# The FFN blocks of f-tiles 16 and 17: seven block products with one pair in place of the plain output product

## The chip, the cores and the metric

The kernel runs on one core of one Trainium2 chip, as one launch. The metric is the device time of that launch in microseconds (us). TensorE is called PE (PEld is its weight load), VectorE DVE, ScalarE ACT, GpSimd POOL and SyncE SP, as the profile calls them.

## The reference, cut to what matters

```python
def swiglu(x, w_in, w_out):
    gate, up = jnp.split(x @ w_in, 2, axis=-1)
    return (jax.nn.silu(gate) * up) @ w_out
...
        x = x + 0.5 * swiglu(rmsnorm(x, ffn1_norm_g[l]), ffn1_w_in[l], ffn1_w_out[l])
...
        x = x + 0.5 * swiglu(rmsnorm(x, ffn2_norm_g[l]), ffn2_w_in[l], ffn2_w_out[l])
    return rmsnorm(x, final_norm_g)
```

There are 1024 tokens, d_model is 1024 and d_ff is 2816, which is 22 tiles of 128 (the f-tiles). Between the two FFNs stands a mixer (mLSTM and a gated MLP) that the change does not touch. All of it is float32.

## The kernel before

Every float32 matrix product is made of three matmuls: each operand is split into a rounded high part and a low part (a cast on ACT, then a subtraction on DVE), and high*high, high*low and low*high are summed in PSUM (`PROD`, `prod`, `split`, `unit`).

An FFN works on the tokens in two halves of 512. Its input product uses, for each f-tile, a scheme with seven block products instead of eight over the 2x2 blocks of (input rows, gate or up) and (input rows, token half). `group(f)` does the five that are left once `first_products` has done two and put them into DRAM; `fetch` brings these back. Four of its sums of weight blocks run on POOL (lines 303 to 305 and 352). It ends with the activated tile for both token halves, `u3` and `c22`.

The output product goes block by block (`BLOCKS`): four blocks of four f-tiles (0 to 15), one of two (16 and 17), and one of four (18 to 21). Blocks with f0 under `FAST` = 16 use seven block products as well: f-tiles are taken in pairs, `group` of the odd tile makes seven operands of the pair (`H`), and `down_fast` runs for each d of 0 to 3 (output tiles d and d+4) the seven products 11, t1, t2, 21, t3, 22, t4, each over two pairs, so 6 matmuls. On the way, the bank of product 11 is copied to a second bank (line 398) into which t2 accumulates, that one is copied to a third (line 408) into which t3 accumulates, and the results leave by ACT copies (lines 404, 412, 427) and DVE additions (418, 422). Each result is added to the residual in DRAM by an accumulating DMA that POOL issues: 16 of 256 KB for a block.

The block (16, 2) is not under `FAST`: `group` only splits `u3` and `c22`, and `down` computes each of the 16 output tiles plainly, with 2 f-tiles times 3 matmuls, an ACT copy (line 440) and the same kind of accumulating DMA (line 441). The last block (18 to 21) goes to `last`, which makes the final sums.

`run` calls the output product of a block after the first group of the next block. So between group 17 and the products of (16, 2) on PE stands group 18, of 60 matmuls, and after them come groups 19, 20 and 21, of 60 each.

The order on each engine is not the order of the code: a scheduler sets it when the program is built, and at run time each engine goes through its own list in order. Tiles come from rotating pools: four raw weight buffers (`raws`), four split weight units (`fw`), eleven [128, 512] temporaries (`tps`), six PSUM banks "mm". A buffer is written again once its last reader is done; an input that an accumulating DMA reads is free when that DMA has landed. The raw loads of a group or a block are issued by SP.

Of the kernel before, what the change touches and what calls it, by code (L numbers as in the profile page):

```python
# [8 lines left out]
F32 = mybir.dt.float32  # L9
F32R = mybir.dt.float32r  # L10
AF = mybir.ActivationFunctionType
ALU = mybir.AluOpType

P = 128
S = 1024
D = 1024
NH = 512
KT = D // P
DFF = 2816
NF = DFF // P  # L20
BLOCKS = [(0, 4), (4, 4), (8, 4), (12, 4), (16, 2), (18, 4)]
FAST = 16
SPAD = 40
MPAD = 24
TMP = 11
# [9 lines left out]
def block_body(ctx, tc, x, ffn1_norm_g, ffn1_w_in, ffn1_w_out, mix_norm_g, w_mix_in, mlstm_conv_w,  # L35
               mlstm_conv_b, mlstm_b_igate, mlstm_b_fgate, mlstm_head_norm_g, sgu_norm_g, sgu_norm_b,
               sgu_w_s, sgu_b_s, w_mix_out, ffn2_norm_g, ffn2_w_in, ffn2_w_out, final_norm_g, out):
    nc = tc.nc
    V, A, PE, G = nc.vector, nc.scalar, nc.tensor, nc.gpsimd
    x = x[0]  # L40
    out = out[0]
# [4 lines left out]
    raws = []  # L46
# [8 lines left out]
    def bank(tag):  # L55
        return psum[tag].tile([P, NH], F32, tag=tag, name=tag)
# [40 lines left out]
    for nm, src in (("g1", ffn1_norm_g), ("gm", mix_norm_g), ("g2", ffn2_norm_g), ("hg", mlstm_head_norm_g),  # L97
                    ("sg", sgu_norm_g), ("sb", sgu_norm_b), ("cb", mlstm_conv_b)):
        n = src.shape[-1] // P
# [47 lines left out]
    def spread():  # L147
        if todo:
            todo.pop(0)()
# [118 lines left out]
    class Ffn:  # L268
# [60 lines left out]
        def group(self, f):  # L329
# [31 lines left out]
            u3 = sg1  # L361
            if f >= FAST:
                self.hs.append((self.part(self.hp, u3), self.part(bigp, c22)))
# [19 lines left out]
            split(src, t)  # L383
            return t

        def down_fast(self, f0, H, acc):
            for d in range(4):
                r = raws[-1].tile([P, 4, 2, P], F32, tag="raw", name="raw")
                for j in range(2):
                    nc.sync.dma_start(out=r[:, :, j, :], in_=self.w_out[f0 * P:(f0 + 4) * P, (4 * j + d) * P:(4 * j + d + 1) * P]  # L390
                                      .rearrange("(k p) c -> p k c", p=P))
                rv = r.rearrange("p (i s) j c -> p i s j c", s=2)
                a11, a12, a21, a22 = rv[:, :, 0, 0, :], rv[:, :, 1, 0, :], rv[:, :, 0, 1, :], rv[:, :, 1, 1, :]
                w = self.unit(a11, 2)
                a = bank("mm")
                self.prod(a, w, H["11"], True, False)
                x = bank("mm")
                A.copy(out=x, in_=a)
                s1 = self.sums(V, a11, a12, a21, a22, 2)
                w = self.unit(s1, 2)  # L400
                b = bank("mm")
                self.prod(b, w, H["t1"], True, True)
                p5 = self.c512()
                A.copy(out=p5, in_=b)
                w = self.unit(a11, 2)
                self.prod(x, w, H["t2"], False, True)
                y = bank("mm")
                A.copy(out=y, in_=x)
                w = self.unit(a12, 2)
                self.prod(a, w, H["21"], False, True)  # L410
                c11 = self.c512()
                A.copy(out=c11, in_=a)
                G.dma_start(out=acc[0][d], in_=c11, accum_op=ALU.add)  # L413
                V.tensor_tensor(out=a12, in0=a12, in1=a11, op=ALU.subtract)
                w = self.unit(a21, 2)
                self.prod(y, w, H["t3"], False, True)
                c22 = self.c512()
                V.tensor_tensor(out=c22, in0=y, in1=p5, op=ALU.add)  # L418
                G.dma_start(out=acc[1][d + 4], in_=c22, accum_op=ALU.add)
                w = self.unit(a12, 2)  # L420
                self.prod(x, w, H["22"], False, True)
                V.tensor_tensor(out=p5, in0=x, in1=p5, op=ALU.add)
                G.dma_start(out=acc[1][d], in_=p5, accum_op=ALU.add)
                w = self.unit(a22, 2)
                self.prod(y, w, H["t4"], False, True)
                c21 = self.c512()
                A.copy(out=c21, in_=y)
                G.dma_start(out=acc[0][d + 4], in_=c21, accum_op=ALU.add)

        def down(self, f0, n, hs, acc):  # L430
            for d in range(0, KT, 2):
                raw = raws[-1].tile([P, n, 2 * P], F32, tag="raw", name="raw")
                nc.sync.dma_start(out=raw, in_=self.w_out[f0 * P:(f0 + n) * P, d * P:(d + 2) * P]
                                  .rearrange("(k p) c -> p k c", p=P))
                for j in range(2):
                    w = self.unit(raw[:, :, j * P:(j + 1) * P], n)
                    for t in range(2):
                        o = self.down_mm(w, n, [h[t] for h in hs], slice(0, NH))
                        xt = self.c512()
                        A.copy(out=xt, in_=o)  # L440
                        G.dma_start(out=acc[t][d + j], in_=xt, accum_op=ALU.add)
                spread()

        def down_mm(self, w, n, hs, ts):
            o = bank("mm")[:, ts]
# [34 lines left out]
        def run(self, src, final, parts, hook):  # L480
            pend = None
            self.fetch(0)
            for bi, (f0, n) in enumerate(BLOCKS):
                hs = self.hs = []
                H = self.H = {k: [] for k in ("11", "21", "22", "t1", "t2", "t3", "t4")}
                for f in range(f0, f0 + n):
                    self.group(f)
                    if pend is not None:
                        pend()
                        pend = None  # L490
                    spread()
                if f0 < FAST:
                    pend = lambda f0=f0, H=H: self.down_fast(f0, H, src)
                elif bi < len(BLOCKS) - 1:
                    pend = lambda f0=f0, n=n, hs=hs: self.down(f0, n, hs, src)
                else:
                    self.last(f0, n, hs, src, final, parts, hook)

# [387 lines left out]
    with f1:  # L886
# [62 lines left out]
        xt = []  # L949
# [125 lines left out]
```

## Time and profile before

| | us |
|---|---|
| median of 3 runs | 2279.01 (2276.77 to 2283.1) |
| the profiled execution | 2283.09 |
| its span | 2281.3 |
| PE busy in the span | 2230.2 (98%) |
| DVE busy | 1488.2 (65%) |
| ACT busy | 1123.0 (49%) |
| POOL busy | 506.3 (22%) |

The span runs from the first to the last instruction of the profiled execution; the launch itself adds 1.8 us. Busy time of PE is that of modelled, pipelined matmuls, so full PE is read best from the starts of matmuls that follow each other. Idle time of an engine that nothing waits for costs nothing.

### The profile page before, as it was taken

Reading aid. Unit: us, or ns where it says so; the run is one execution under the profiler, and the core shown is the slowest. Engines: PE = TensorE matmul, PEld = TensorE weight load, DVE = VectorE, ACT = ScalarE, POOL = GpSimd, SP = SyncE. Lnnn points to the kernel's source line nnn. Section 1 sums busy time; section 2 is a strip of 40 time slices with the busy share of each in tenths; the row PEclk is TensorE's granted clock in tenths of the full one; section 3 lists DMA queues with packets and bytes.
Section 4 is the critical chain, followed back from the end, with each engine's and each line's share of the span. In section 5 each row is a group of like instructions: output and inputs, shape, how many; then the busy total and the mean of one; then the engine's idle time right before and its main releaser. Section 6 shows DMA issues by size and latency. Waiting matters only on the chain. (4 is left out here: it accounts for less than half of the span.)

```text
span 2281.3 us, 30658 instructions
## 1 busy us (share of the span) xinstructions
PE 2230.2 (98%) x10979; PEld 1868.4 (82%) x10979; DVE 1488.2 (65%) x2563; ACT 1123.0 (49%) x1924; POOL 506.3 (22%) x557
## 2 busy tenths in 40 slices
PE   7999999999999999999999999999999999999998
PEld 5888788788879888888889888888788787878877
DVE  6748777686565757656656576555726786877456
ACT  6645555544534446454434554543644555555542
POOL 3342534424520000000000000000215334253430
PEclk8999999999999999999999999999999999999999
DMA  8853756737753234233343253333864557375663
GB/s 274 268 180 101 154 115 157 135 106 147 176 194 100 77 92 129 84 92 85 101 146 95 84 166 85 91 92 126 269 198 147 111 141 154 97 161 109 149 159 111
DMA packets 331512, 311.51 MB, mean 137 GB/s; under 512 B 19160, under 2 KB 279896, under 8 KB 331360
## 3 DMA queue, kind: packets, MB, share of 16 engines
q1 hardware_dynamic: 292608, 217.20, 32.2%
q0 software_dynamic: 38752, 92.36, 18.5%
q8 instruction: 86, 1.41, 0.3%
q14 instruction: 66, 0.54, 0.1%
HBM read 223.48 MB, written 86.02 MB: 136 GB/s over the span
## 5 line engine op out<-in xcount | busy, mean ns | idle before, releaser
L297 PE MATMUL mm<-b,fw 128*128 128x512 f32 x2640 | 605.6, 391 | 9.6 <-ACT mm L342 4.9
L297 PEld LDWEIGHTS mm<-b,fw 128*128 128x128 f32 x2640 | 496.6, 188 | 116.7 <-ACT mm L342 7.4
L162 PE MATMUL mm<-xn,w 128*128 128x512 f32 x2304 | 546.6, 391 | 0.0
L291 DVE TENSOR_TENSOR fw<-raw,fw 128x512 fp32r<-128x512 f32 (+1 forms) x472 | 328.7, 703 | 297.4 <-ACT fw L290 295.7
L162 PEld LDWEIGHTS mm<-xn,w 128*128 128x128 f32 x2304 | 427.1, 188 | 82.8
L290 ACT CAST fw<-raw 128x512 fp32r<-128x512 f32 (+1 forms) x472 | 248.3, 527 | 174.3 <-PE mm L297 139.1
L297 PE MATMUL mm<-h,fw 128*128 128x512 f32 x1344 | 313.6, 393 | 5.2 <-DVE c L418 4.4
L297 PEld LDWEIGHTS mm<-h,fw 128*128 128x128 f32 x1344 | 248.5, 188 | 68.9 <-ACT fw L290 8.3
L138 DVE TENSOR_TENSOR w<-raw,w 128x1024 fp32r<-128x1024 f32 (+3 forms) x160 | 178.5, 1116 | 163.9 <-ACT w L137 163.4
L297 PE MATMUL mm<-xn,fw 128*128 128x512 f32 x1056 | 246.2, 394 | 3.6 <-ACT xn L195 2.1
L137 ACT CAST w<-raw 128x1024 fp32r<-128x1024 f32 (+3 forms) x160 | 153.9, 964 | 178.8 <-PE mm L162 85.6
L297 PEld LDWEIGHTS mm<-xn,fw 128*128 128x128 f32 x1056 | 199.5, 190 | 49.1 <-ACT xn L195 3.7
L176 PE MATMUL mm<-w,xn 128*128 128x256 f32 x1344 | 163.9, 282 | 0.0
L176 PEld LDWEIGHTS mm<-w,xn 128*128 128x128 f32 x1344 | 161.8, 189 | 1.4 <-issue 0.5
L256 POOL DMA_DIRECT2D xs<-t x16 | 8.7, 544 | 641.8 <-DVE t L253 641.1
L195 ACT CAST h<-c 128x512 fp32r<-128x512 f32 x136 | 82.4, 621 | 73.4 <-DVE c L371 17.6
L196 DVE TENSOR_TENSOR h<-c,h 128x512 fp32r<-128x512 f32 x136 | 101.8, 776 | 10.0 <-ACT h L195 8.9
L303 POOL TENSOR_TENSOR s<-raw 128x512 f32<-128x512 f32 x44 | 62.7, 1424 | 156.5 <-DMA raw<-in_ffn_w_in_dram 121.8
L448 PE MATMUL mm<-h,wl 128*128 128x512 f32 (+1 forms) x480 | 95.9, 353 | 0.0
L413 POOL DMA_DIRECT2D xd<-c x32 | 28.0, 876 | 298.9 <-ACT fw L290 262.2
L162 PE MATMUL po<-mh,w 128*128 128x512 f32 x384 | 87.5, 389 | 0.0
L448 PEld LDWEIGHTS mm<-h,wl 128*128 128x128 f32 x480 | 77.3, 189 | 12.0 <-ACT h L195 0.5
(258 smaller groups left out, 2625.4 us busy)
## 6 DMA issues: line engine op xcount, KB each, us to landing
raw<-in_ffn_w_in_dram SPq DMA_DIRECT2D x264, 256.0 KB, 3.4
raw<-in_w_mix_in_dram SPq DMA_DIRECT2D x96, 512.0 KB, 3.7
xd<-c POOLq DMA_DIRECT2D x160, 256.0 KB, 5.3
eb<-early POOLq DMA_DIRECT2D x88, 256.0 KB, 2.8
c<-eb SPq DMA_DIRECT2D x88, 256.0 KB, 5.2
raw<-in_ffn_w_out_dram SPq DMA_DIRECT2D x72, 256.0 KB, 3.2
raw<-in_w_mix_in_dram SPq DMA_DIRECT2D x32, 384.0 KB, 3.5
xl<-xd POOLq DMA_DIRECT2D x32, 256.0 KB, 4.1
```

The lines of the kernel that those rows point to most:

```text
L137: A.copy(out=w[:, 0, 0:n, :], in_=raw[:, 0:n, :])
L138: V.tensor_tensor(out=w[:, 1, 0:n, :], in0=raw[:, 0:n, :], in1=w[:, 0, 0:n, :].bitcast(F32), op=ALU.subtract)
L162: PE.matmul(out=banks[j], lhsT=w[:, a, i, j * P:(j + 1) * P], rhs=act[k][:, b, ts], start=(k == first and pi == 0), stop=(k == last and pi ...
L176: PE.matmul(out=o, lhsT=act[k][:, b, t * P:(t + 1) * P], rhs=w[:, a, i, :], start=(t % 2 == 0 and k == 0 and pi == 0), stop=(t % 2 == 1 an ...
L195: A.copy(out=dst[:, 0, :], in_=src)
L196: V.tensor_tensor(out=dst[:, 1, :], in0=src, in1=dst[:, 0, :].bitcast(F32), op=ALU.subtract)
L290: A.copy(out=w[:, 0], in_=src)
L291: V.tensor_tensor(out=w[:, 1], in0=src, in1=w[:, 0].bitcast(F32), op=ALU.subtract)
L297: PE.matmul(out=bank, lhsT=w[:, x, i, :], rhs=t[:, y, :], start=(start and i == 0 and pi == 0), stop=(stop and i == len(b) - 1 and pi == 2 ...
L303: G.tensor_tensor(out=s1, in0=a21, in1=a22, op=ALU.add)
L413: G.dma_start(out=acc[0][d], in_=c11, accum_op=ALU.add)
L448: PE.matmul(out=o, lhsT=w[:, x, i, :], rhs=hs[i][:, y, ts], start=(i == 0 and pi == 0), stop=(i == n - 1 and pi == 2))
```

## The change

`FAST` becomes 18, so the block of f-tiles 16 and 17 takes the path of the first four blocks, with one pair: `down_fast` gets the number of f-tiles `n`, its weight units hold n // 2 blocks (128x128 instead of 128x256 where n is 2), and each of the seven products has 3 matmuls. `down` goes away. `group` of f-tile 17 makes the seven operands of the pair where it split two tiles.

```diff
-FAST = 16
+FAST = 18
...
-        def down_fast(self, f0, H, acc):
+        def down_fast(self, f0, n, H, acc):
             for d in range(4):
-                r = raws[-1].tile([P, 4, 2, P], F32, tag="raw", name="raw")
+                r = raws[-1].tile([P, n, 2, P], F32, tag="raw", name="raw")
                 for j in range(2):
-                    nc.sync.dma_start(out=r[:, :, j, :], in_=self.w_out[f0 * P:(f0 + 4) * P, (4 * j + d) * P:(4 * j + d + 1) * P]
+                    nc.sync.dma_start(out=r[:, :, j, :], in_=self.w_out[f0 * P:(f0 + n) * P, (4 * j + d) * P:(4 * j + d + 1) * P]
                                       .rearrange("(k p) c -> p k c", p=P))
...
-                w = self.unit(a11, 2)
+                w = self.unit(a11, n // 2)
...
-                s1 = self.sums(V, a11, a12, a21, a22, 2)
-                w = self.unit(s1, 2)
+                s1 = self.sums(V, a11, a12, a21, a22, n // 2)
+                w = self.unit(s1, n // 2)
...
-        def down(self, f0, n, hs, acc):
-            for d in range(0, KT, 2):
...
-                    w = self.unit(raw[:, :, j * P:(j + 1) * P], n)
-                    for t in range(2):
-                        o = self.down_mm(w, n, [h[t] for h in hs], slice(0, NH))
-                        xt = self.c512()
-                        A.copy(out=xt, in_=o)
-                        G.dma_start(out=acc[t][d + j], in_=xt, accum_op=ALU.add)
...
                 if f0 < FAST:
-                    pend = lambda f0=f0, H=H: self.down_fast(f0, H, src)
-                elif bi < len(BLOCKS) - 1:
-                    pend = lambda f0=f0, n=n, hs=hs: self.down(f0, n, hs, src)
+                    pend = lambda f0=f0, n=n, H=H: self.down_fast(f0, n, H, src)
                 else:
                     self.last(f0, n, hs, src, final, parts, hook)
```

In the built program the lines after `down` move up by 14 to 16; the lines of `group` and `down_fast` up to 428 keep their numbers.

PE in the second FFN, in the block of f-tiles 16 and 17: before, one pair of output tiles for both token halves (mm_ is the PSUM bank, h_ an operand tile, fw_ a weight unit).

```order
L448 MATMUL mm_18812<-h_18175,fw_18809 128x512 x3
L448 MATMUL mm_18812<-h_18644,fw_18809 128x512 x3
L448 MATMUL mm_18822<-h_18178,fw_18809 128x512 x3
L448 MATMUL mm_18822<-h_18647,fw_18809 128x512 x3
L448 MATMUL mm_18835<-h_18175,fw_18832 128x512 x3
L448 MATMUL mm_18835<-h_18644,fw_18832 128x512 x3
```

The same place with the change: d = 2 of the four, from its product 11 (mm_19013) to the start of the next d (mm_19082); mm_18969 is the last bank of d = 1.

```order
L297 MATMUL mm_19013<-h_18272,fw_19010 128x512
L297 MATMUL mm_18969<-h_18757,fw_18998 128x512 x3
L297 MATMUL mm_19013<-h_18272,fw_19010 128x512 x2
L297 MATMUL mm_19026<-h_18742,fw_19023 128x512 x3
L297 MATMUL mm_19017<-h_18750,fw_19032 128x512 x3
L297 MATMUL mm_19013<-h_18738,fw_19040 128x512 x3
L297 MATMUL mm_19038<-h_18746,fw_19050 128x512 x3
L297 MATMUL mm_19017<-h_18754,fw_19059 128x512 x3
L297 MATMUL mm_19082<-h_18272,fw_19079 128x512
L297 MATMUL mm_19038<-h_18757,fw_19067 128x512 x3
```

A weight unit served two independent banks with 12 matmuls, and no bank was read before it was complete; now a unit serves 3 matmuls, and the banks of one d (19013, 19017, 19038) are copies of each other, with 3 matmuls between the end of one and the start of the next.

ACT at the same place: before, two output tiles for both halves (L440 empties a bank; L290 is the cast of a weight unit).

```order
L440 COPY c_18819<-mm_18812 128x512
L440 COPY c_18829<-mm_18822 128x512
L290 CAST fw_18905<-raw_18903 128x256
L440 COPY c_18842<-mm_18835 128x512
L440 COPY c_18852<-mm_18845 128x512
L290 CAST fw_18928<-raw_18903 128x256
```

With the change, d = 2:

```order
L290 CAST fw_19010<-raw_19007 128x128
L290 CAST fw_19023<-s_19019 128x128
L427 COPY c_19004<-mm_18969 128x512
L398 COPY mm_19017<-mm_19013 128x512
L290 CAST fw_19032<-raw_19007 128x128
L290 CAST fw_19040<-raw_19007 128x128
L404 COPY c_19030<-mm_19026 128x512
L290 CAST fw_19050<-raw_19007 128x128
L408 COPY mm_19038<-mm_19017 128x512
L290 CAST fw_19059<-raw_19007 128x128
L412 COPY c_19046<-mm_19013 128x512
L290 CAST fw_19067<-raw_19007 128x128
```

The cast of the unit for t2 (fw_19032) stands behind the copy L398, which waits for product 11; casts and copies alternate on ACT, 7 and 5 for 21 matmuls, where 2 and 4 served 24.

POOL, end of the block in the second FFN: before (xd are the residual tiles in DRAM, raw_19060 and raw_19063 the weights of group 20).

```order
L441 DMA xd114_145<-c_18877 128x512
L303 TENSOR_TENSOR s_19072<-raw_19060,raw_19063 128x512
L441 DMA xd105_138<-c_18890 128x512
L304 TENSOR_TENSOR raw_19060<-raw_19060 128x4x128
L441 DMA xd115_146<-c_18900 128x512
L305 TENSOR_TENSOR raw_19060<-s_19072,raw_19060 128x4x128
L441 DMA xd106_139<-c_18915 128x512
L352 TENSOR_TENSOR raw_19063<-raw_19063,raw_19060 128x4x128
```

With the change (raw_19145 and raw_19148 are the weights of group 19, raw_19254 those of group 20):

```order
L428 DMA xd106_139<-c_19073 128x512
L305 TENSOR_TENSOR raw_19145<-s_19157,raw_19145 128x4x128
L352 TENSOR_TENSOR raw_19148<-raw_19148,raw_19145 128x4x128
L413 DMA xd103_136<-c_19115 128x512
L419 DMA xd117_148<-c_19125 128x512
L423 DMA xd113_144<-c_19099 128x512
L428 DMA xd107_140<-c_19142 128x512
L303 TENSOR_TENSOR s_19266<-raw_19254,raw_19257 128x512
```

The sums of group 19 now stand where those of group 20 stood, behind the accumulating DMAs of d = 2, and those of group 20 behind all sixteen.

## Rows read from the trace of the kernel before

**Rows 1.** The page: span, and the busy time of PE.

```profile
span 2281.3 us, 30658 instructions
...
PE 2230.2 (98%) x10979; PEld 1868.4 (82%) x10979; DVE 1488.2 (65%) x2563; ACT 1123.0 (49%) x1924; POOL 506.3 (22%) x557
```

**Rows 2.** Timeline, PE, both FFNs: start, us, engine, line, operation, count [idle before].

```profile
570.99 21.92 PE L448 MATMUL mm<-h,fw 128*128 128x512 f32 x96
592.75 40.98 PE L297 MATMUL mm<-b,fw 128*128 128x512 f32 x180
633.57 6.69 PE L448 MATMUL mm<-h,wl 128*128 128x512 f32 x28
...
2145.60 21.92 PE L448 MATMUL mm<-h,fw 128*128 128x512 f32 x96
2167.36 11.04 PE L297 MATMUL mm<-b,fw 128*128 128x512 f32 x48
2183.09 32.69 PE L297 MATMUL mm<-b,fw 128*128 128x512 f32 x132 [4.69 <-DVE c L351]
2215.62 4.63 PE L448 MATMUL mm<-h,wl 128*128 128x512 f32 x19
```

**Rows 3.** Stretches: us, busy PE, PEld, DVE, ACT, POOL, granted clock, DMA share, GB/s.

```profile
2180.00:2185.00 5.00, 1.92 (x5) 1.56 (x6) 5.00 (x5) 0.97 (x3) 5.00 (x5) 0.66 0.94 148
```

**Rows 4.** Timeline, second FFN, around group 20's weights after the block.

```profile
2173.32 1.28 POOL L303 TENSOR_TENSOR s<-raw 128x512 f32<-128x512 f32 x1 [9.71 <-DMA raw<-in_ffn_w_in_dram]
2177.03 1.89 POOL L305 TENSOR_TENSOR raw<-s,raw 128x512 f32<-128x512 f32 x1
2178.95 0.62 ACT L290 CAST fw<-raw 128x512 fp32r<-128x512 f32 x1 [2.38 <-POOL raw L305]
2182.26 0.68 DVE L351 TENSOR_TENSOR c<-mm,c 128x512 f32<-128x512 f32 x1
```

**Rows 5.** Timeline, first FFN, the same wait of POOL.

```profile
591.30 1.29 POOL L303 TENSOR_TENSOR s<-raw 128x512 f32<-128x512 f32 x1 [2.78 <-DMA raw<-in_ffn_w_in_dram]
```

**Rows 6.** Raw weight loads by SP, 2141 to 2185: issue to landing.

```profile
DMA to landing us min/median/max: 3.0/4.9/13.2
```

**Rows 7.** Timeline, second FFN, f-tiles 12 to 15 with two pairs.

```profile
2078.84 27.80 PE L297 MATMUL mm<-h,fw 128*128 128x512 f32 x120
2107.26 11.29 PE L297 MATMUL mm<-h,fw 128*128 128x512 f32 x48 [0.63 <-DVE c L418]
2118.39 1.99 PE L297 MATMUL mm<-b,fw 128*128 128x512 f32 x8
```

**Rows 8.** Timeline, its start: the first copy, the cast behind it, and a DVE release.

```profile
2080.40 0.57 ACT L398 COPY mm<-mm 128x512 f32<-128x512 f32 x1
2080.88 0.41 ACT L290 CAST fw<-raw 128x256 fp32r<-128x256 f32 x1
...
2106.43 0.68 DVE L418 TENSOR_TENSOR c<-mm,c 128x512 f32<-128x512 f32 x1
```

**Rows 9.** Groups by line and form, whole span: count, busy us, mean ns, idle before.

```profile
L290 ACT CAST fw<-raw 128x512 fp32r<-128x512 f32 x264 | 163.4, 620 | 109.2 <-PE mm L297 92.6 <-POOL raw L305 8.3 <-issue 6.6
L290 ACT CAST fw<-raw 128x256 fp32r<-128x256 f32 x208 | 84.8, 408 | 65.1 <-PE mm L297 46.6 <-DVE fw L291 15.9 <-DVE raw L414 2.5
L418 DVE TENSOR_TENSOR c<-mm,c 128x512 f32<-128x512 f32 x32 | 21.9, 683 | 0.0
L291 DVE TENSOR_TENSOR fw<-s,fw 128x256 fp32r<-128x256 f32 x32 | 13.3, 416 | 0.0
L239 DVE TENSOR_SCALAR t<-ident,rstd 128x128 f32<-128x128 f32 x16 | 3.6, 283 | 0.1
```

**Rows 10.** Timeline, DVE beside POOL's sums, second FFN, third d of the block.

```profile
2101.70 4.35 DVE L291 TENSOR_TENSOR fw<-raw,fw 128x256 fp32r<-128x256 f32 x4
2101.76 1.90 POOL L305 TENSOR_TENSOR raw<-s,raw 128x512 f32<-128x512 f32 x1
2103.74 1.37 POOL L352 TENSOR_TENSOR raw<-raw 128x512 f32<-128x512 f32 x1
```

More of the change, by code (lines that the diff above doesn't have):

```diff
@@ L404, in down_fast @@
                 A.copy(out=p5, in_=b)
-                w = self.unit(a11, 2)
+                w = self.unit(a11, n // 2)
                 self.prod(x, w, H["t2"], False, True)
@@ L408, in down_fast @@
                 A.copy(out=y, in_=x)
-                w = self.unit(a12, 2)
+                w = self.unit(a12, n // 2)
                 self.prod(a, w, H["21"], False, True)
@@ L414, in down_fast @@
                 V.tensor_tensor(out=a12, in0=a12, in1=a11, op=ALU.subtract)
-                w = self.unit(a21, 2)
+                w = self.unit(a21, n // 2)
                 self.prod(y, w, H["t3"], False, True)
@@ L419, in down_fast @@
                 G.dma_start(out=acc[1][d + 4], in_=c22, accum_op=ALU.add)
-                w = self.unit(a12, 2)
+                w = self.unit(a12, n // 2)
                 self.prod(x, w, H["22"], False, True)
@@ L423, in down_fast @@
                 G.dma_start(out=acc[1][d], in_=p5, accum_op=ALU.add)
-                w = self.unit(a22, 2)
+                w = self.unit(a22, n // 2)
                 self.prod(y, w, H["t4"], False, True)
@@ L428, in down_fast @@
                 G.dma_start(out=acc[0][d + 4], in_=c21, accum_op=ALU.add)
-        def down(self, f0, n, hs, acc):
-            for d in range(0, KT, 2):
[L432 to L435, printed above, removed]
-                    w = self.unit(raw[:, :, j * P:(j + 1) * P], n)
-                    for t in range(2):
-                        o = self.down_mm(w, n, [h[t] for h in hs], slice(0, NH))
-                        xt = self.c512()
-                        A.copy(out=xt, in_=o)
-                        G.dma_start(out=acc[t][d + j], in_=xt, accum_op=ALU.add)
-                spread()
         def down_mm(self, w, n, hs, ts):
@@ L482, in run @@
             self.fetch(0)
-            for bi, (f0, n) in enumerate(BLOCKS):
+            for f0, n in BLOCKS:
                 hs = self.hs = []
```

## The prediction

> **What bounds the kernel now.** I read the page first: PE is busy for 2230 of 2281 us [rows 1], so time is won where PE gets fewer matmuls and lost where PE has to wait. Then PE's timeline around the changed block in both FFNs [rows 2]. In the first FFN its 96 matmuls run from 570.99 to 592.75, that is 21.76 us or 0.2267 us each, and the next 180 follow without a gap (592.75 to 633.57 is 40.82 us, again 0.2267 each). In the second FFN the block is the same, 2145.60 to 2167.36, but after 48 more matmuls PE waits 4.69 us, and the 180 take until 2215.62: 48.26 us, 7.46 more than at full pace. 4.69 of these are the wait; the rest is a lower clock, since the granted clock between 2180 and 2185 is 0.66 [rows 3], a mixture of the 2.4 and the 1.2 GHz level, after that wait.
>
> The views around that wait tell its cause. POOL's first sum for group 20 waits 9.71 us for its raw weights; its third ends at 2178.9, the cast behind it starts at 2178.95, and the addition L351 of group 19, which PE needs, ends at 2182.94 [rows 4]. One of the loads of that stretch took 13.2 us to land, where the median is 4.9 [rows 6]. In the first FFN the same sum starts 20.3 us after the block's first matmul (591.30) [rows 5] instead of 27.7, and nothing stalls. So what comes after this block hangs on a margin of some 5 us.
>
> **What the change removes.** 12 of 96 matmuls in each FFN, 24 in all: 24 x 0.2267 = 5.44 us. This is all that PE gains, and it is 0.24%. A measurement of this kernel can tell about 0.3%, or 6.8 us, from no change.
>
> **What it adds, beside other work.** In each FFN: 3 more splits of [128, 512] and 4 subtractions for the pair's operands, and on SP 8 loads of half the size for 4. The operands are made while PE does the 60 matmuls of group 18 (13.6 us), and an earlier pair has the same cover; I take 0 for them, and without that cover they would cost some 5 us (7 DVE instructions of 0.68). The sixteen accumulating DMAs stay.
>
> **What it adds on PE's path.** Now the banks of one d depend on each other. How long such a step takes is read from the blocks with two pairs [rows 7, 8]: the first product starts at 2078.84, so its sixth matmul starts at 2079.97; the copy L398 starts at 2080.40, 0.43 us later, takes 0.57, and lets the cast behind it start 0.48 after itself. From L418's end (2107.11) to the matmul that waited for it (2107.26) are 0.15 us. A cast takes 0.62 us for 512 columns and 0.41 for 256, so for 128 I estimate 0.30; a subtraction 0.42 for 256, and 0.28 for 128 like the nearest row of that size [rows 9]. A product of 3 matmuls covers 0.68 us, one of 6 covered 1.36. Counted from the start of the last matmul before the step:
>
> - t2 needs the copy and the cast behind it: 0.43 + 0.48 + 0.30 = 1.21, and 0.15 to 0.3 to the matmul. PE is covered to 0.23 + 0.68 = 0.91: about 0.5 idle.
> - t3 needs only its copy: 1.00 and 0.1 to 0.15. Cover again 0.91: 0.2 idle.
> - t4 must wait until L418 has read its bank: 0.43 + 0.68 + 0.15 = 1.26, with 1.13 covered by product 22 and one matmul of the next d. Then DVE has the low part of t4's unit, L422 (0.68, after product 22) and only then the low part for the next d's product 11, whose third matmul needs it: together 0.45 idle.
>
> That makes 1.15 us for a d, 4.6 for a block, 9.2 for both FFNs. The nearest check from below: with two pairs, 168 matmuls take 2118.39 - 2078.84 = 39.55 us [rows 7] where 38.08 would be full pace, so even there 1.47 us go, and each step had 0.68 us more cover. I keep 0.5 for a d (2.0 for a block) as the lower bound, and 1.6 (6.4) as the upper.
>
> **DVE beside POOL.** While POOL did two sums (1.90 and 1.37 us), four DVE subtractions of 0.42 us took 4.35 [rows 10]: 1.09 each, a loss of 2.7 us for 3.3 us of POOL. In that block PE lost only 0.63 to it [rows 7]. In the new one, 11 of DVE's 13 instructions for a d are of this kind, two SBUF inputs each, and PE has no product in hand. Two of group 19's four sums stand before the DMAs of d = 2, so inside the block: 3 us of POOL, up to 2.5 us lost on DVE. I take 1.5 for a block; bounds 0 (all of it falls into DVE's idle time) and 3.
>
> By the Trainium skill, page SBUF — State Buffer, section Who interferes with whom, such a pair of instructions shares one read interface, and the one that comes second is blocked until the first ends. The trace agrees for the most part: about one subtraction passed for each POOL instruction or each gap between two. By the strict rule 1.5 us would be 3, inside the bounds.
>
> **What moves.** Before, a raw buffer of the block was free after two weight units, the first of them before the block began; now it is free after seven, at the end of its d. The second half of group 19's weights can then be loaded only after d = 1, some 11.5 us into the block; it lands 5 later, POOL's first two sums take 3, four DMA issues of about 1 us stand before the third (the order of POOL shows it), and that third sum, 1.9, ends at about 25 to 26, when the block of 19.0 + 4.6 + 1.5 = 25.1 us ends. With the cast behind it I put 1.5 us of PE idle there, bounds 0 and 4. For group 20 it is the same with less margin: its last load comes after the block's last d and behind two fetches that wait for accumulating DMAs, so a stall of the kind of rows 4, of about 2.5 us, is likely in both FFNs. That is +2.5 in the first and 2.5 - 7.46 = -5.0 in the second, together -2.5; the bounds are -7.5 (no stall any more) and +7.5 (a full one in both).
>
> **The sum**: -5.4 + 9.2 + 3.0 (DVE beside POOL) + 3.0 (group 19) - 2.5 = +7.3 us on the profiled execution's 2283.09: 2290.4. The median of the runs shown is 4.1 us below that execution, which I lay to a smaller stall after the block in those runs; with a stall of 3.4 there the last term is +1.6, and the sum on 2279.01 is 2290.4 too. I forecast **2290**, slower by 0.5%.
>
> **The rivals.**
>
> *The steps are mostly hidden* (no difference). If ACT and DVE hand over faster, with 0.5 us of idle for a d, and nothing else is lost, it is 2283.1 - 5.4 + 4.0 = 2281.7; with 1.5 us for POOL it is 2284.7. For it: for the 4.76 us of a d, DVE has 11 x 0.28 + 2 x 0.68 = 4.4 us of work, and ACT 7 x 0.30 + 5 x 0.58 = 5.0 less the 0.09 by which each starts before the one ahead has ended [rows 8], about 3.9; so neither is overbooked. Against it: the order on ACT puts the cast for t2 behind the copy.
>
> *The late load goes* (faster). The accumulating DMAs keep the queues full after the block now; if they spread and group 20 gets its weights in time, the 7.46 us of the second FFN fall away. With 0.25 us of idle for a d: 2283.1 - 5.4 - 7.5 + 2.0 = 2272.2, which is 0.3% below the median. This is the point from which it decides: both have to hold, steps under 0.25 us and no stall. For it: the first FFN shows that the stall need not be there. Against it: the raw buffers come free later than before.
>
> *The clock falls inside the block* (much slower). At 25 us for 19.0 us of matmuls PE is busy for 76% of it. If that brings the clock to its lower level for some 30 matmuls, each takes 0.43 instead of 0.23: 6 us more in each FFN, 2302. Against it: the low clock before came only after 4.69 us of idle in one piece.
>
> *The change does nothing*: excluded, the order of PE shows 84 matmuls for 96, and the sixteen DMAs of another kind.
>
> **How the numbers follow.** My case 0.44, at 2286 to 2303; hidden steps 0.32; late load gone 0.12; clock 0.12. So slower by more than 0.3% (above 2285.8) 0.56, within 0.32, faster (below 2272.2) 0.12. The range is 2274 to 2303: below, the bound with the steps at 2.0 a block and no stall at all (2283.1 - 5.4 + 4.0 - 7.5 = 2274.2); above, about what all terms at their upper bounds in one FFN give (2290.4 + 1.8 + 1.5 + 2.5 + 5.0 = 2301). That leaves out about 0.1 on either side. My case alone would be 2286 to 2303.
>
> **What would show it.** The block should run 84 matmuls in 23 to 27 us, with repeated PE idle of 0.2 to 0.7 us before t2, t3, t4 and product 11, released by L398 or L290 on ACT and L418 or L291 on DVE; groups of DVE subtractions of 128x128 that take about 1 us beside POOL; PE idle at the start of group 19 released by the chain from L305. If the 84 matmuls take under 21 us, the steps are hidden and my main term is wrong; if the stall after the block is gone in both FFNs, the term for group 20 is.

## The result and the profile after

The changed kernel takes 2302.8 us (median of 6 runs, 2300.31 to 2308.45), the kernel before 2281.06 on the same chip (2276.77 to 2289.07). The ratio is 1.0094, with a 95% interval of 1.0079 to 1.011: **slower by 0.9%, some 21 us**. The profiled execution took 2303.2 us.

The page of the changed kernel, as [rows 1]:

```profile
PE 2239.5 (97%) x10955; PEld 1865.0 (81%) x10955; DVE 1516.9 (66%) x2665; ACT 1134.1 (49%) x1978; POOL 505.2 (22%) x557
```

PE has 24 matmuls fewer and is busy 9.3 us longer. PE's timeline around both blocks, as [rows 2] (start, us, engine, line, operation, count, [idle before <-who ended it]):

```profile
573.36 7.16 PE L297 MATMUL mm<-h,fw 128*128 128x512 f32 x27
580.86 5.57 PE L297 MATMUL mm<-h,fw 128*128 128x512 f32 x21 [0.34 <-ACT fw L290]
586.60 5.55 PE L297 MATMUL mm<-h,fw 128*128 128x512 f32 x21 [0.17 <-ACT fw L290]
592.34 3.27 PE L297 MATMUL mm<-h,fw 128*128 128x512 f32 x12 [0.18 <-ACT fw L290]
...
603.93 44.27 PE L297 MATMUL mm<-b,fw 128*128 128x512 f32 x180 [7.20 <-ACT fw L290]
648.03 12.32 PE L434 MATMUL mm<-h,wl 128*128 128x512 f32 x53
...
2161.93 7.19 PE L297 MATMUL mm<-h,fw 128*128 128x512 f32 x27
...
2192.06 43.81 PE L297 MATMUL mm<-b,fw 128*128 128x512 f32 x180 [6.14 <-ACT fw L290]
2235.71 4.62 PE L434 MATMUL mm<-h,wl 128*128 128x512 f32 x19
```

In the first FFN the block runs from 573.36 to the wait's beginning at 603.93 - 7.20 = 596.73, so 23.37 us for 84 matmuls against 21.76 for 96. Then PE waits 7.20 us in one piece, and the next 180 matmuls take 44.10 us against 40.82. Together +1.61 + 7.20 + 3.28 = +12.1 us. In the second FFN the block takes 23.99 us (+2.23) and the wait 6.14, and the 180 matmuls 43.65 against 48.26, since before they held the stall of [rows 2] (-4.61): +3.8 us. The other 4.2 us between the two profiled executions lie in stretches that the change doesn't touch.

The stretches around the wait in the first FFN (us, busy PE, PEld, DVE, ACT, POOL, granted clock, DMA share, GB/s), as [rows 3]:

```profile
591.00:597.00 6.00, 5.36 (x20) 3.22 (x19) 3.18 (x10) 4.15 (x11) 1.18 (x1) 1.00 0.85 199
597.00:604.00 7.00, 0.07 (x1) 0.07 (x1) 0.09 (x1) 0.74 (x2) 6.84 (x8) 0.72 0.87 155
604.00:609.00 5.00, 4.97 (x11) 3.51 (x12) 2.93 (x4) 1.92 (x4) 4.08 (x5) 0.50 1.14 239
```

The clock is whole in the block, falls during the wait, and the 11 matmuls of 604 to 609 run at 0.50, the 1.2 GHz level: so the 3.28 us belong to the wait. What PE waits for is seen on POOL and ACT there (timeline, as [rows 4]):

```profile
595.82 1.28 POOL L303 TENSOR_TENSOR s<-raw 128x512 f32<-128x512 f32 x1 [8.18 <-DVE c L418]
597.18 1.26 POOL L304 TENSOR_TENSOR raw<-raw 128x512 f32<-128x512 f32 x1
598.38 0.88 POOL L413 DMA_DIRECT2D xd<-c  x1
598.97 1.18 POOL L419 DMA_DIRECT2D xd<-c  x1
599.51 1.53 POOL L423 DMA_DIRECT2D xd<-c  x1
600.05 1.88 POOL L428 DMA_DIRECT2D xd<-c  x1
600.62 2.60 POOL L305 TENSOR_TENSOR raw<-s,raw 128x512 f32<-128x512 f32 x1
...
603.26 0.62 ACT L290 CAST fw<-raw 128x512 fp32r<-128x512 f32 x1 [7.95 <-POOL raw L305]
```

Group 19's first sum starts only at 595.82, 22.5 us after the block's first matmul. Before, it started 5.9 us after it (570.99 in [rows 2]):

```profile
576.86 1.48 POOL L303 TENSOR_TENSOR s<-raw 128x512 f32<-128x512 f32 x1
```

The changed kernel's idle time there is put down to L418, which had just ended. But it was the load of the weights: in the second FFN, with the same code, the sum started while L418 was still running, and its wait is put down to the load.

```profile
2183.55 0.69 DVE L418 TENSOR_TENSOR c<-mm,c 128x512 f32<-128x512 f32 x1 [0.52 <-PE mm L297]
2183.95 1.27 POOL L303 TENSOR_TENSOR s<-raw 128x512 f32<-128x512 f32 x1 [8.25 <-DMA raw<-in_ffn_w_in_dram]
```

Then the four DMAs of d = 2 stand between L304 and L305, and the cast that PE needs comes behind L305. The second half of these weights was issued from 584.41 on, 11 us into the block, in two loads. The loads of 570 to 600, and below them these two alone, landed after these times, as [rows 6]:

```profile
DMA to landing us min/median/max: 3.1/6.6/10.8
DMA to landing us min/median/max: 10.1/10.5/10.8
```

So the theory (A) after the result: a weight buffer that comes free late, a load that lands late, POOL's queue behind it, and the low clock behind the wait. The rivals: the wait has nothing to do with buffers; the block's own steps or DVE beside POOL are the loss.

One measure serves all runs: from where the block's first matmul was due (its start less the wait ahead of it) to the last block's first matmul. For the first and second FFN it was 62.6 and 70.0 us before, 74.7 and 73.8 after. Where an edit added code, the lines in a run's rows lie a little further down.

### The profile page after: what moved, and what is told of

Same layout as the page of the kernel before. It is cut to its first block, busy times and chain, and to the rows that moved or that the text cites. A ratio compares the mean times of both kernels' runs of the same rounds, so it can differ in the third digit from the quotient of the medians.

```text
span 2301.4 us, 30812 instructions
## 1 busy us (share of the span) xinstructions
PE 2239.5 (97%) x10955; PEld 1865.0 (81%) x10955; DVE 1516.9 (66%) x2665; ACT 1134.1 (49%) x1978; POOL 505.2 (22%) x557
## 3 DMA queue, kind: packets, MB, share of 16 engines
q8 instruction: 86, 1.41, 0.3%
## 5 line engine op out<-in xcount | busy, mean ns | idle before, releaser
L291 DVE TENSOR_TENSOR fw<-raw,fw 128x512 fp32r<-128x512 f32 (+2 forms) x504 | 330.9, 665 | 287.8 <-ACT fw L290 285.3
L297 PE MATMUL mm<-h,fw 128*128 128x512 f32 x1512 | 359.7, 395 | 9.3 <-DVE c L418 4.0
L297 PEld LDWEIGHTS mm<-h,fw 128*128 128x128 f32 x1512 | 277.7, 188 | 89.8 <-ACT fw L290 13.9
L290 ACT CAST fw<-raw 128x512 fp32r<-128x512 f32 (+2 forms) x504 | 254.5, 509 | 193.7 <-PE mm L297 135.3
L195 ACT CAST h<-c 128x512 fp32r<-128x512 f32 x142 | 85.5, 621 | 73.5 <-DVE c L371 18.3
L413 POOL DMA_DIRECT2D xd<-c x40 | 34.9, 873 | 348.5 <-ACT fw L290 311.9
L303 POOL TENSOR_TENSOR s<-raw 128x512 f32<-128x512 f32 x44 | 61.5, 1397 | 166.6 <-DMA raw<-in_ffn_w_in_dram 105.7
```

The costliest lines, as they stand in the source:

```text
L195: A.copy(out=dst[:, 0, :], in_=src)
L290: A.copy(out=w[:, 0], in_=src)
L291: V.tensor_tensor(out=w[:, 1], in0=src, in1=w[:, 0].bitcast(F32), op=ALU.subtract)
L297: PE.matmul(out=bank, lhsT=w[:, x, i, :], rhs=t[:, y, :], start=(start and i == 0 and pi == 0), stop=(stop and i == len(b) - 1 and pi == 2 ...
L303: G.tensor_tensor(out=s1, in0=a21, in1=a22, op=ALU.add)
```

## The experiments

**The block's weights in tiles of their own.** The two halves of group 19 then need not wait for the block's buffers.

```diff
-                r = raws[-1].tile([P, n, 2, P], F32, tag="raw", name="raw")
+                if n > 2:
+                    r = raws[-1].tile([P, n, 2, P], F32, tag="raw", name="raw")
+                elif d % 2 == 0:
+                    own = bigp.tile([P, 2, n, 2, P], F32, tag="big", name="own")
+                if n == 2:
+                    r = own[:, d % 2]
```

> The changed kernel, but the block's output weights are loaded into two tiles of the 16-tile operand pool instead of the four raw buffers, so that the weights of groups 19 and 20 do not wait for the block. Theory A (the raw buffers come free late, so group 19 starts late): the 7.2 and 6.1 us of PE idle before group 19 and the low clock behind them (3.3 and 3.0 us) go, the 84 matmuls still take about 23 us, or up to 26 if POOL's sums now fall into the block; total near 2283, 0.1% above the kernel before. Rival B (the accumulating DMAs hold the transfers back whatever the buffers are): idle before group 19 or 20 of 4 us or more stays, total above 2293. Rival C (the loss is mostly inside the block, in the steps between dependent banks): total above 2295 with no idle before group 19.

Measured: 2298.2 us, ratio 1.0081 (1.0066 to 1.0095); 72.0 and 73.6 us for the two FFNs. PE in the first FFN:

```profile
575.19 8.38 PE L297 MATMUL mm<-h,fw 128*128 128x512 f32 x27 [2.28 <-ACT fw L290]
...
601.09 1.20 PE L297 MATMUL mm<-h,fw 128*128 128x512 f32 x4 [0.92 <-DVE fw L291]
...
604.37 40.66 PE L297 MATMUL mm<-b,fw 128*128 128x512 f32 x178 [0.51 <-DVE fw L291]
```

The forecast of 2283 us (theory A) was missed by 15, and the time and the missing wait are those of rival C. The wait before group 19 is down to half a microsecond, and the 178 matmuls behind it run at full pace, 0.228 us each: the low clock went with the wait. But the scheduler now puts the block's loads behind those of groups 19 and 20 on SP, so PE waits 2.28 us at the block's start, and d = 2 and 3 are torn up by idle times that DVE ends. The groups of DVE in that run, first over 577 to 589.5 (d = 0 and 1), then over 589.5 to 604 (count, busy us, mean ns, idle before):

```profile
L291 DVE TENSOR_TENSOR fw<-own,fw 128x128 fp32r<-128x128 f32 x13 | 3.6, 287 | 3.4 <-ACT fw L290 3.4
L419 DVE TENSOR_TENSOR own<-own 128x128 f32<-128x128 f32 x2 | 0.6, 288 | 0.0
...
L291 DVE TENSOR_TENSOR fw<-own,fw 128x128 fp32r<-128x128 f32 x11 | 6.2, 587 | 2.2 <-ACT fw L290 2.2
L419 DVE TENSOR_TENSOR own<-own 128x128 f32<-128x128 f32 x2 | 3.3, 1631 | 0.1
```

The same operations take two to six times as long where POOL does its sums for groups 19 and 20. So without the late buffer the wait before group 19 goes, and the price of early weights is that the sums meet the block. Whether the loss inside the block is the steps (rival C) or POOL is left to the run without sums below.

**The same, with two d side by side.** The products of d and d + 1 alternate, so that one covers the steps of the other; t1's product goes to a bank of "ml".

```diff
-            for d in range(4):
...
+            for d in range(0, 4, step):
...
+                live = [self.down_d(d + i, f0, n, H, acc, r) for i, r in enumerate(rs)]
+                while live:
+                    live = [g for g in live if next(g, 0) is None]
```

> As the run with its own weight tiles, and two values of d run side by side, product by product, with the bank of product t1 taken from the other PSUM pool: between two dependent products of one d stands one more product of the other. Theory A with the steps as the only loss inside the block: the 84 matmuls in 19.2 to 20.5 us instead of 23.2, no idle before group 19; total 2270 to 2277. Rival D (ACT and DVE are the bound of the block, not the order of the steps): the 84 matmuls still take 22 us or more, total 2280 to 2286.

Measured: 2297.14 us, ratio 1.0081 (1.0065 to 1.0096); 73.5 and 71.3 us.

```profile
580.15 8.53 PE L297 MATMUL mm<-h,fw 128*128 128x512 f32 x36
588.52 0.84 PE L297 MATMUL ml<-h,fw 128*128 128x512 f32 x3
...
597.34 1.65 PE L297 MATMUL mm<-h,fw 128*128 128x512 f32 x3 [1.60 <-DVE fw L291]
```

Where POOL is quiet, 36 matmuls run through in 8.37 us from start to start, 0.2325 each: with a second d in hand the steps are hidden. The second pair, beside POOL's sums, loses it all again, and neither forecast of the time held (2270 to 2277, or 2280 to 2286).

**The kernel before, with such tiles for the plain block.** Could its stall of the second FFN be had away in that manner?

```diff
-                raw = raws[-1].tile([P, n, 2 * P], F32, tag="raw", name="raw")
+                if d % 4 == 0:
+                    own = bigp.tile([P, 2, n, 2 * P], F32, tag="big", name="own")
+                raw = own[:, d // 2 % 2]
```

> The kernel before, with the plain block's output weights in two tiles of the operand pool instead of the raw buffers. If the wait of 4.69 us behind the block in the second FFN (7.46 with the low clock) came from late raw buffers, it goes and the total is 2274 to 2278; if it came from the accumulating DMAs alone, the wait stays in some executions and the total is within 2 us of the kernel before.

Measured: 2292.5 us, ratio 1.0053 (1.0035 to 1.007); 72.1 and 72.2 us. It is slower, not faster. PE waits 2.94 us for the block's late loads, and again in group 20:

```profile
611.16 0.59 ACT L337 COPY mm<-c 128x512 f32<-128x512 f32 x1 [6.82 <-DMA c<-eb]
...
614.25 7.99 PE L297 MATMUL mm<-b,fw 128*128 128x512 f32 x27 [2.95 <-DVE c L351]
```

Here it is the fetch of the early products (c<-eb) that comes late, since on SP it stands behind weight loads that wait for a buffer. One wait is bought with two others.

**Seven products in one FFN only.** `FAST` is 18 for the first FFN and 16 for the second, and in the last run the reverse.

> Seven products with one pair in the first FFN alone; the second FFN keeps the plain block. Theory A: block about 23.2 us in the first FFN, 7 us of idle before group 19 and 3 us of low clock behind it, so 11 to 13 us more than before: about 2293, and the second FFN as before. If the cost lay in something that the two FFNs share, it would be 0 or 21 us.

Measured, the first FFN only: 2290.58 us, ratio 1.0052 (1.0031 to 1.0073). The first FFN takes 74.0 us, with the wait as in the changed kernel:

```profile
605.53 43.42 PE L298 MATMUL mm<-b,fw 128*128 128x512 f32 x180 [7.40 <-ACT fw L291]
```

The second, plain as before, takes 66.9 us and has a stall of 2.48 us instead of 4.69 in [rows 2].

> The seven block products in the second FFN only, the first FFN as before. Theory G (the two FFNs' losses add, and the second's is larger than the two profiled executions show, 73.8 us against 70.0, because the plain block's stall of group 20 in the second FFN differs from execution to execution: 7.5 us with its low clock in the profile of before, 4.5 in that of the run with the first FFN only): ratio 1.003 to 1.0055, 2288 to 2293 us, so that with the first FFN's 11 to 12 us the whole 21.7 us is reached. Rival H (3.8 us is the second FFN's share, and the rest of the 21.7 us comes from elsewhere, where both are changed together): ratio 1.0005 to 1.0025, 2282 to 2287 us. In the trace: the wait before group 19 of the second FFN 5.5 to 7 us, low clock behind it, no stall of group 20.

Measured, the second FFN only: 2291.56 us, ratio 1.0038 (1.0022 to 1.0054); 63.5 and 75.0 us, and the wait somewhat longer than expected:

```profile
2174.09 44.26 PE L298 MATMUL mm<-b,fw 128*128 128x512 f32 x180 [7.33 <-ACT fw L291]
```

The two losses, 0.52% and 0.38%, add up to the 0.9% of the whole change: theory G. By that ratio the second FFN costs some 8.7 us (the medians lie 11.4 apart), not the 3.8 of the two profiled executions. A reason at hand is that the stall which it replaces is not the same in every execution (4.69 and 2.48 us in the two traces with the plain block there); that this makes up the whole difference is not shown.

**Without the accumulating DMAs of d = 2**: POOL's queue by itself.

```diff
-                G.dma_start(out=acc[0][d], in_=c11, accum_op=ALU.add)
+                if not (n == 2 and d == 2):
+                    G.dma_start(out=acc[0][d], in_=c11, accum_op=ALU.add)
```

(and so for the three others)

> The change, with the four accumulating DMAs of d = 2 of the block of f-tiles 16 and 17 left out (the output lacks these four products). They stand on POOL between L304 and L305 of group 19 and cost it some 2.2 to 2.4 us there. Theory A (the wait before group 19 is the late landing of its second weight half, and behind it POOL's queue): the landing stays near 10 us, L305 starts right after L304, and PE's wait before group 19 falls by about 2.2, from 7.2 to 5.0 us in the first FFN and from 6.1 to 3.9 in the second. Rival B (the queue on POOL costs nothing, the landing alone sets the wait): both waits stay within 0.5 us of 7.2 and 6.1.

Measured: 2293.09 us in one run; 69.3 and 70.7 us.

```profile
595.20 1.27 POOL L303 TENSOR_TENSOR s<-raw 128x512 f32<-128x512 f32 x1 [7.72 <-DMA raw<-in_ffn_w_in_dram]
596.55 1.27 POOL L304 TENSOR_TENSOR raw<-raw 128x512 f32<-128x512 f32 x1
597.90 1.26 POOL L305 TENSOR_TENSOR raw<-s,raw 128x512 f32<-128x512 f32 x1
...
599.86 42.80 PE L297 MATMUL mm<-b,fw 128*128 128x512 f32 x180 [2.69 <-ACT fw L290]
```

The waits fall to 2.69 and 4.07 us. Since the load's landing against the block's end differs by a microsecond between executions, the clean measure is from L303's start to PE's: 8.11 us in both FFNs of the changed kernel, 4.66 and 4.65 here. So the queue costs 3.45 us, more than the 2.2 that I put down, and the rows as [rows 4] tell how: the records of the four DMA issues overlap, but their ends (599.26, 600.15, 601.04, 601.93) lie 0.89 apart, so POOL does them one after the other. L305's record of 2.60 us begins while the last of them still runs; it ends at 603.22, 1.29 behind it, as long as the 1.26 that it takes here. Four issues of 0.88 are 3.5 us. POOL's wait for the load stays: theory A, with a larger queue.

**Without all sixteen accumulating DMAs of the block**, the same edit with the condition n == 2.

> The change, with all sixteen accumulating DMAs of the block left out in both FFNs (the output lacks the block's products). Theory A1 (the second half of group 19 lands after 10.5 us and not 5 because the accumulates' 4 MB stand in front of it on the DMA engines): it lands in 3 to 6 us, group 19's sums on POOL start by 591 on the time axis of the change's run, the wait before group 19 falls under 1 us and the 180 matmuls behind take 40.7 to 41.0 us; the sums then run beside d = 2 and 3 and stretch these by 1 to 4 us. Rival A2 (the landing is long by the weight loads themselves): it stays at 8 us or more and the wait at 4 us or more.

Measured: 2286.97 us in one run; 68.2 and 66.4 us. (Of one run the total says little: the kernel before took 2276.85 to 2290.31 us beside it.) The loads of 570 to 600:

```profile
DMA to landing us min/median/max: 2.9/3.3/4.0
```

POOL and PE in the first FFN:

```profile
586.83 1.30 POOL L303 TENSOR_TENSOR s<-raw 128x512 f32<-128x512 f32 x1 [34.71 <-ACT mm L408]
...
597.46 11.30 PE L297 MATMUL mm<-b,fw 128*128 128x512 f32 x48
610.09 30.21 PE L297 MATMUL mm<-b,fw 128*128 128x512 f32 x132 [1.33 <-DVE c L351]
```

Theory A1: the median landing is 3.3 us, none takes more than 4.0, group 19's sums start at 586.8, and the wait before group 19 is gone. The accumulates are what made the load slow to land. So the wait needs two things at once, a load that is issued late and accumulates beside it; without either it goes, and about half of it, 3.45 us, is the queue on POOL. The same sixteen accumulates were there before the change: what it added is the late issue. The sums now fall into the block, which takes 25.5 and 24.7 us instead of 23.4 and 24.0, and group 20 waits a little (1.33 and 0.42 us), so that the 180 matmuls take 42.7 and 41.7 us, which I had not expected. How much of the DMA time they take is in the queues of the changed kernel from 578 to 597 (packets, MB, time of the packets as a share of 16 engines), q0 being POOL's accumulates and q1 SP's loads:

```profile
q0 software_dynamic: 1152, 2.10, 66.8%
q1 hardware_dynamic: 3180, 1.58, 30.6%
```

2.10 MB are 8 accumulates of 256 KB: 0.668 x 19 us / 8 = 1.59 us of all sixteen engines for one, so 25.4 us for the sixteen of a block that lasts 23 to 24. By the Trainium skill, page DMA: Bandwidth & Descriptors, section Queues, rings and completion order, a DMA engine takes turns between its queues, packet by packet. The rows agree in that both queues move packets in the same stretch; how the turns are shared they don't show. The two loads of group 19's second half, issued from 584.41 on, were through at 594.5 and 595.7, the last of the eight accumulates issued up to 587 at 594.9.

**Own tiles, without the sums of groups 19 and 20**: does DVE suffer from POOL, or from the block itself?

```diff
-            s1 = self.sums(G, a11, a12, a21, a22, 4)
+            s1 = a22 if f in (19, 20) else self.sums(G, a11, a12, a21, a22, 4)
...
-            G.tensor_tensor(out=a12, in0=a12, in1=a11, op=ALU.subtract)
+            if f not in (19, 20):
+                G.tensor_tensor(out=a12, in0=a12, in1=a11, op=ALU.subtract)
```

> As the run with the block's weights in tiles of their own, but groups 19 and 20 of both FFNs leave out their four sums on POOL (PE, ACT and DVE do the same number of operations on other operands, so the output is wrong in these groups). Theory C (in that run d = 2 and 3 took longer because DVE's operations ran 3 to 7 times their 0.28 us beside POOL's sums): all four d take 5.7 to 5.8 us each, no idle of PE above 0.4 us inside the block, block about 23.5 us behind its start wait of 2.3 (0.5 of it low clock), and no low clock behind it. Rival D (the block's own steps or its accumulates slow the later d): d = 2 and 3 still take 7 us or more together with idles above 0.5 us.

Measured: 2291.23 us in one run; 68.2 and 68.0 us.

```profile
585.28 5.57 PE L297 MATMUL mm<-h,fw 128*128 128x512 f32 x21 [0.17 <-ACT fw L290]
591.03 5.55 PE L297 MATMUL mm<-h,fw 128*128 128x512 f32 x21 [0.18 <-ACT fw L290]
596.76 3.29 PE L297 MATMUL mm<-h,fw 128*128 128x512 f32 x12 [0.18 <-ACT fw L290]
...
600.99 41.22 PE L297 MATMUL mm<-b,fw 128*128 128x512 f32 x180
```

The stretch of 579 to 582 in it (columns as [rows 3]):

```profile
579.00:582.00 3.00, 3.00 (x10) 2.33 (x9) 0.78 (x4) 1.81 (x6) 0.00 (x0) 0.56 0.00 0
```

Theory C: each d takes 5.7 us, to the end. The start was underrated: the first 27 matmuls take 9.00 us instead of 7.16, 1.8 us for the low clock (0.56 in that stretch) behind the 2.28 us wait, where I put 0.5. So the 5.7 us a d are the steps, and what lies above it in the run with own tiles comes from POOL's sums. By the Trainium skill, page SBUF — State Buffer, section Who interferes with whom, an instruction of DVE with two SBUF inputs contends with POOL's reads; the rows agree (1631 ns for L419 beside the sums, 288 without them).

**The kernel before, with fewer buffers for the plain block**: d and d + 2 share one raw buffer, so that groups 19 and 20 get theirs earlier; then the same in the second FFN only.

```diff
-                raw = raws[-1].tile([P, n, 2 * P], F32, tag="raw", name="raw")
+                if d % 4 == 0:
+                    two = raws[-1].tile([P, 2, n, 2 * P], F32, tag="raw", name="raw")
+                raw = two[:, d // 2 % 2]
```

> The kernel before, the plain block's loads of d and d + 2 in one raw buffer (two buffers a block instead of four), so that groups 19 and 20 get their buffers earlier. Theory E (the second FFN's stall of 4.7 us and the low clock behind it, 7.5 us in all, come from group 20's buffer): the stall goes and nothing takes its place, 2270 to 2275 us. Rival F (earlier loads bring POOL's sums or the loads of the early products into the block's time, as in the run with own tiles for the plain block): a wait of 2 us or more shows in either FFN and the time is 2278 to 2292 us.

> The kernel before, with d and d + 2 of the plain block in one raw buffer in the second FFN only (the first, with four raw buffers, had no stall). The first FFN as before (62.6 us from block start to the last block's first matmul), the second 64 us instead of 70. If nothing is lost elsewhere, 6 us less than before: 2273 to 2276 us, ratio 0.997 to 0.998. Rival (the gain of a stall is lost in the last stage or in the spread of single runs): ratio above 0.999.

(Both FFNs have four raw buffers. Three for the second FFN, which the first text of the next pair says, is the mixer's number and was a mistake of mine.) Measured: 2279.22 us, ratio 0.9991 (0.9977 to 1.0005), with 63.7 and 64.0 us; for the second FFN only 2280.97 us, ratio 1.0003 (0.9988 to 1.0018), with 67.0 and 64.3 us. Group 20's wait in the second FFN of the first of them, and in the first FFN, whose code is the old one, of the second:

```profile
2180.45 30.50 PE L297 MATMUL mm<-b,fw 128*128 128x512 f32 x132 [0.82 <-DVE c L351]
```

```profile
609.89 31.77 PE L298 MATMUL mm<-b,fw 128*128 128x512 f32 x132 [2.56 <-DVE c L352]
```

In the second FFN the 4.69 us shrink to 0.82, 6 us with the clock, but the medians don't show it: both forecasts (2270 to 2275, 2273 to 2276) failed, and the second run's rival held. The second row shows why: in the first FFN, where code and the order of every engine are those of the kernel before, the stall was 0 in [rows 2], 0.62 in the run with the seven products in the second FFN only, 2.56 here. It comes and goes from execution to execution, so one trace can overrate it. Neither version beats the kernel before by what can be measured.

**The change, with two d in one buffer** (raw buffers; in the second FFN the second pair in a tile of its own), and then **with two d side by side as well**. The diff is against the run with own tiles.

```diff
-                    own = bigp.tile([P, 2, n, 2, P], F32, tag="big", name="own")
+                    own = bigp.tile([P, 2, n, 2, P], F32, tag="big", name="own") if self.n == 2 and d else \
+                        raws[-1].tile([P, 2, n, 2, P], F32, tag="raw", name="raw")
```

> The change, with two d of the block in one buffer (raw buffers; in the second FFN, which has three raw buffers instead of four, the second pair in a tile of its own), so that both halves of group 19 take buffers that group 18 frees, and their loads stand behind the block's on SP. Theory A (buffers): group 19's second half is issued before the block's first matmul or in its first 3 us, no wait above 0.5 us before the block, none above 1 us before group 19, no low clock behind it; group 19's sums on POOL run beside d = 2 and 3, block 24.5 to 26 us; group 20, whose buffers are now the block's, waits up to 2 us. Time 2284 to 2290 us. Rival (the wait only moves, to group 20): a wait of 4 us or more there with low clock, 2292 us or more.

> As the run before it, and two d side by side with t1's product in a bank of ml, so that while one d's steps run the other's matmuls cover them. Theory: the first pair at full pace, 9.6 us; the second pair beside group 19's sums, 11 to 14 us; block 21 to 23.5 us against 22 of the plain one; no wait of group 19; time 2278 to 2284 us. Rival (DVE has no room, both pairs are bound by it): block 24 us or more, 2285 us or more.

Measured: 2297.88 us, ratio 1.0073 (1.0053 to 1.0094), with 76.4 and 69.7 us; and 2300.65 us, ratio 1.0078 (1.0059 to 1.0097), with 77.5 and 69.2 us. Both theories failed, and the times are those of the rivals. The first of the two, its weight loads from 595 to 612:

```profile
DMA to landing us min/median/max: 6.8/10.5/10.9
```

and its timeline there, POOL and PE:

```profile
610.69 1.25 POOL L304 TENSOR_TENSOR s<-raw 128x512 f32<-128x512 f32 x1 [10.34 <-DMA raw<-in_ffn_w_in_dram]
...
617.27 5.05 PE L298 MATMUL mm<-b,fw 128*128 128x512 f32 x13 [7.65 <-DVE c L352]
```

No wait stands before group 19 any more; in the first FFN, where the block's two buffers are now group 20's, it stands before group 20, 7.65 us, and 10.27 us with two d side by side. In the second FFN, with one buffer more, neither is there (no idle time above 1.41 us), but the block takes 27.8 and 24.6 us beside POOL's sums. So the wait goes to whichever group takes over the block's buffers.

## Why the prediction was right, and where its sum was not

I forecast slower, 2290 us; it is slower, 2302.8, at the very end of the range, which went to 2303. That the time still lies in it is luck: the term that failed went far over its upper bound, and two others came out at their lower bounds. Point by point:

- **The matmuls.** 84 in place of 96, at 0.2267 us where nothing stops them. Right.
- **The steps on PE's path.** I put 4.6 us a block, 1.15 for a d. The period of a d is 5.74 us against 4.76 at full pace, 0.98; 84 x 0.2267 = 19.04 from 23.37 and 23.99 leaves 4.3 and 4.9. By the starts of the matmuls from 580.86 to 586.60, 0.46 of it stand at t2, 0.24 at t3 and 0.28 in the rest, where I put 0.5, 0.2 and 0.45. Right, and the run without sums shows that they are there even when POOL is quiet, so the rival of hidden steps fell. They could be hidden by a second d, as the first pair of the run with two d side by side shows.
- **DVE beside POOL.** I put 1.5 us a block, with sums inside the block. In the changed kernel itself the sums came too late to meet it, but for one subtraction at the end of the second FFN's block; without the accumulates they did, and the block grew by 2.1 and 0.7 us. The term had the right size in a place where the next term removed it.
- **Group 19.** "With the cast behind it I put 1.5 us of PE idle there, bounds 0 and 4." This is the step that failed: 7.2 and 6.1 us, and 3.3 and 2.9 us of low clock behind it. The chain was the one that I had named (buffer after d = 1, landing, POOL's queue, third sum, cast), and its start at 11 us was right; but I took 5 us for the landing, the median of [rows 6], where the row's own maximum was 13.2 and the load stood among accumulates: it took about 10.5. So the matmul behind the chain came at 30.6 us instead of 26.6, and the block was over at 23.4 instead of 25.1: the two make the 5.7 us between 1.5 and 7.2. The queue on POOL was not the error: I counted four issues of about 1 us and 1.9 for the third sum, and it was 3.5 and 1.3, since the 1.9 of [rows 4] overlaps the issue in front of it. And to a wait of that length belongs the clock, which I had read in [rows 3] for the stall of before and not put into this term.
- **Group 20.** "A stall ... of about 2.5 us, is likely in both FFNs." None came: the 180 matmuls run in one piece. That its load had the time behind the long wait for group 19 is my reading. It is not that its load is safe: in three of the runs without the wait before group 19, group 20 waits, by 0.42 to 10.27 us. In the second FFN the old stall's 7.46 us went whole, where I had left 2.5 of them.
- **The rivals.** The late load did not go but moved ahead by one group. The rival of the falling clock gave nearly the right time, 2302, by a mechanism that did not occur: inside the block the clock is 1.00, though PE is busy for some 80% of it.

The sum with what was measured: in the first FFN +1.6 (block) + 7.2 + 3.3 = 12.1; in the second +2.2 + 6.1 + 2.9 - 7.5 = 3.8 with rounding, or 8.7 by the ratio of the run that changes it alone. In the terms of the prediction it is -5.4 + 9.2 + 0 (DVE beside POOL) + 19.5 (group 19 with its low clock) - 7.5 = +15.8 where I had +7.3; the other 4.2 of the two profiled executions stay unexplained. The saved 5.4 us are less than the 9.2 of the steps, and in the run without any accumulates, with the wait before group 19 gone, the blocks still took 25.5 and 24.7 us against 21.76 of the plain one. So in this form the block itself loses; all that the edit could win is the old stall of the second FFN.

What stays open: why the profiled executions differ by up to 8 us where no code differs (from the first FFN's last block to the second FFN's block 1509.0 to 1517.4 us, without a relation to the edits); and whether two d side by side, with the sums kept out of the block and buffers for all, would win: no such kernel was run, and none with more raw buffers in the pool.

## What to carry to other kernels

Before matmuls are taken out of a block, see for how long its instructions hold the buffers that the next loads need: a buffer that was free after two weight units and is now free at the end of its d cost more here than twelve matmuls are worth. Take for the landing of a load not its median but what it was beside the same other transfers: sixteen accumulates filled the DMA engines for the whole block, and each rearrangement that was run moved the loss, to the block's start, to group 20 or into the block beside POOL's sums. And where a stall is costed, add what the low clock behind it takes, some 3 us here for one of 6 to 7 us. A record that begins while the one in front of it on its engine still runs is read from the end of that one.

## What the runs showed of the hardware that I had not expected

An accumulating DMA of 256 KB took 1.59 us of all sixteen DMA engines, by the share of its queue; of the loads beside them, 1.58 MB or six of 256 KB, one took 0.306 x 19 / 6 = 0.97. With no loads beside them, from 580 to 595 of the run with own tiles, it was 1.69 (8 of them in 90.2% of 15 us). Four DMA issues in a row on POOL ended 0.89 us apart though their records overlap, and the sum behind them 1.29 us after the last, in both FFNs. And behind a wait of 2.28 us the clock was low too (0.56 in the stretch of 579 to 582), which cost 1.8 us over 27 matmuls, in the run with own tiles and no sums.
